# A hybrid RG-LRU / RWKV-7 layer: where the forward substitution of the second half of each pair's chunks runs

## The chip, the cores and the metric

One core of one Trainium2 chip runs the kernel. The metric is the device time of one execution in microseconds (us), a median over several runs. The engines are named as in the profile: PE is TensorE, with its weight loads as PEld; DVE is VectorE; ACT is ScalarE; POOL is GpSimd; SP is SyncE, which issues the DMAs.

## What is computed

One decoder layer over 512 tokens of width 2048. After a normalization with a conditioned shift and scale (adaLN), one projection feeds two groups of heads. The first group is a gated linear recurrence (RG-LRU). The second is RWKV-7 time mixing: 16 heads of 64 features, each with a 64 x 64 state. An output projection, a residual add, a SwiGLU sub-layer and a last normalization follow. The part that matters here is the RWKV-7 recurrence:

```python
def step(state, inp):
    r_t, d_t, k_t, v_t, kk_t, a_t = inp
    sa = jnp.einsum('bhvk,bhk->bhv', state, -kk_t)
    state = (state * d_t[:, :, None, :]
             + sa[..., None] * (kk_t * a_t)[:, :, None, :]
             + v_t[..., None] * k_t[:, :, None, :])
    y_t = jnp.einsum('bhvk,bhk->bhv', state, r_t)
    return state, y_t
```

## The kernel before

Tokens lie along the free dimension, features along the 128 partitions. Every large product is written as three matmuls on operands that were split into a high and a low part (L124, L125, L126); for that each weight tile is loaded (L115), its high part is made on ACT (L105) and its low part on DVE (L106, `wlo`). There are three buffers for the split weights.

The recurrence is computed in chunks of 64 tokens. Two heads make a pair (8 pairs); a pair has 8 chunks, built in two halves of four chunks (`rwkv_half`, hf 0 and hf 1). Within a chunk the step for `sa` is a triangular system, and `inverse` (L750) makes the inverse of I - A for the eight triangular blocks of a half (four chunks, two heads):

- L633 makes the products on PE, L635 masks them into `gb` on DVE, L637 and L639 gather the diagonal 32-blocks into `dg`, and L757 transposes these so that one 32-block lies in one partition (`at`).
- L762 to L766 are the forward substitution. Step s multiplies column s of A with row s of the inverse found so far (L764, into `pr`, shown as `rw_xp`) and adds the product to the rows below (L766, into `x`). There are 31 steps of two instructions, and each instruction takes the result of the one before it. Over the 31 steps an instruction has 31 down to 1 rows and 1 to 4 columns, 920 elements per partition in all.
- L768 and L771 transpose the result back (`xn`, `xs`). L775 copies it on POOL into the block-diagonal operand `xt` (four instructions). L783 and L793 on PE make the lower left blocks.

The chain of a pair (`rwkv_chain`, L666) then takes the eight chunks one after the other. It needs `xt` (L701) and hands the state on through DVE (L720 or L722, `rw_s`, read by PE at L696).

The order of the program is made in two stages. `weave` (L145) writes the steps of five streams (the chains, both halves, the streams' common work and the adaLN columns) into one program by a table of latencies, and fills in the large products as filler wherever no stream is due. A scheduler then puts the instructions of each engine in one list, by its own estimates, and sets the semaphores. At run time each engine goes through its list from top to bottom. POOL's list before holds memsets, the copies at L616 (`bd_a`) and those at L775.

Of the kernel before, what the change touches and what calls it, by code (L numbers as in the profile page):

```python
# [8 lines left out]
F32 = mybir.dt.float32  # L9
# [3 lines left out]
ALU = mybir.AluOpType  # L13
AX = mybir.AxisListType
PSUM = bass.MemoryType.PSUM
DRAM = bass.MemoryType.DRAM

P = 128
S = 512
# [7 lines left out]
C = 64  # L27
# [6 lines left out]
# latencies (us) that weave() goes by when it orders steps; they bear on the order only  # L34
HOP = 1.10                      # a small product, its copy out of PSUM
LM1, LM2, LM3 = 4.2, 6.8, 9.0   # the steps of rwkv_main
LH0 = 4.8                       # rwkv_half's operands
INVLAT = 30.2                   # substitution in the diagonal blocks
LSN = 1.79                      # the next state
MODLAT = (4.0, 3.8, 2.0)        # a quarter of a column of mod, by kind  # L40

# columns of the packed per-feature vectors (one column holds 128 features)
# [14 lines left out]
# columns of the constants (shapes alone)  # L57
# [29 lines left out]
class Layer:  # L87
# [24 lines left out]
    def load_split(self, src, n):  # L112
        """src: DRAM [128, n] -> (hi, lo) float32r tiles [128, n]"""
        raw = self.wp.tile([P, self.wc], F32, tag="raw", name="wraw", bufs=self.wb[0])
        self.nc.sync.dma_start(out=raw[:, :n], in_=src)  # L115
        hi = self.wp.tile([P, self.wc], F32R, tag="whi", name="whi", bufs=self.wb[1])
        lo = self.wp.tile([P, self.wc], F32R, tag="wlo", name="wlo", bufs=self.wb[1])
        with self.tc.high_priority():
            self.split_into(hi[:, :n], lo[:, :n], raw[:, :n])
        return hi, lo  # L120
# [7 lines left out]
    def gemm_steps(self, ps, src, acts):  # L128
        """ps[128, S] = W^T acts, src: DRAM [128, nk * 128], acts: list of (hi, lo); yields after each k"""
        nk = len(acts)  # L130
        kp = self.wc // P
        for k0 in range(0, nk, kp):
            kn = min(kp, nk - k0)
            hi, lo = self.load_split(src[:, k0 * P:(k0 + kn) * P], kn * P)
            for k in range(kn):
                sl = slice(k * P, (k + 1) * P)
                self.mm3(ps, (hi[:, sl], lo[:, sl]), acts[k0 + k], k0 + k == 0, k0 + k == nk - 1)
                yield
# [6 lines left out]
    def weave(self, streams, filler):  # L145
        """Traces the next step of the first stream that can run, a step of filler when none can.
        A stream yields (its last step's us on the tensor engine, the us until the next can run,
        what must hold in the trace before that); filler yields None or such a condition."""
        t = 0.0
        live = [[g, 0.0, None] for g in streams]  # L150
        fcond = None
        while live:
            for st in live:
                if st[1] <= t and (st[2] is None or st[2]()):
                    try:
                        with self.tc.issue_after(self.pe):
                            dur, lat, st[2] = next(st[0])
                        t += dur
                        st[1] = t + lat
                    except StopIteration:  # L160
                        live.remove(st)
                    break
            else:
                if filler is not None and (fcond is None or fcond()):
                    try:
                        fcond = next(filler)
                        t += 0.65
                    except StopIteration:
                        filler = None
                else:  # L170
                    t = min(st[1] for st in live if st[2] is None or st[2]())

# [1 line left out]
    def mod_pair(self, j):  # L174
        """columns j and j + 16"""
        nc = self.nc
        part = self.small.tile([P, 2], F32, tag="adapart", name="adapart", bufs=2)
        for h in range(2):
            t = self.ada.tile([P, D], F32, tag="ada", name="ada", bufs=4)
            nc.sync.dma_start(out=t, in_=self.i["w_ada"][j + 16 * h])  # L180
            nc.vector.scalar_tensor_tensor(out=t, in0=t, scalar=1.0, in1=self.cbc, op0=ALU.mult,
                                           op1=ALU.mult, accum_out=part[:, h:h + 1])
        o = _VOFF["b_ada"] + j
        nc.vector.tensor_tensor(out=self.mod[:, j:j + 17:16], in0=part, in1=self.vecs[:, o:o + 17:16],
                                op=ALU.add)

    def mod_steps(self, js, pool, tags):
        """the same for many columns, a quarter of c at a time"""
# [22 lines left out]
    def mod_scale(self, col, sc, g):  # L211
        """col = g * (1 + mod[:, sc])"""
        self.nc.vector.scalar_tensor_tensor(
            out=col, in0=self.mod[:, sc:sc + 1], scalar=1.0, in1=g, op0=ALU.add, op1=ALU.mult)

    def square(self, acc, x, k, pool):
        """acc += x * x"""
        if k == 0:
            self.nc.scalar.activation(out=acc, in_=x, func=AF.Square)
        else:  # L220
            t = pool.tile([P, S], F32, tag="ft", name="sqt", bufs=2)
            self.nc.scalar.activation(out=t, in_=x, func=AF.Square)
            self.nc.vector.tensor_tensor(out=acc, in0=acc, in1=t, op=ALU.add)

    def norm(self, acc, tag):
        """1 / rms of each token, in all partitions (PSUM), from sums of squares by partition"""
# [16 lines left out]
    def modulate(self, x, col, rstd, sh, lo=None):  # L243
        """hi, lo of x * col * rstd + sh"""
# [54 lines left out]
    def mixing(self):  # L299
# [3 lines left out]
        with ExitStack() as ctx:  # L303
            self.open_ada(ctx)
            with tc.tile_pool(name="xs", bufs=1) as xs:
# [16 lines left out]
                # seven tiles stay in PSUM, four more take turns in the last bank by quarters of K  # L322
# [43 lines left out]
    def rwkv_weave(self, kvr0, kvr1, u0):  # L366
# [16 lines left out]
        def filler():  # L383
# [15 lines left out]
            # half of the channels through the output projection  # L399
# [45 lines left out]
    def project(self, ys, half, *tags):  # L445
        """x1 += g_m * (ys through their half of w_out)"""
# [29 lines left out]
    def rwkv_setup(self, ctx):  # L476
# [4 lines left out]
        # zero at the first token of each chunk  # L481
# [3 lines left out]
        # block-diagonal operands (two heads); what lies off the blocks stays zero  # L485
# [7 lines left out]
    def lora_act(self, m, ps, pool):  # L493
        """what the second products of the low ranks take, the parts of a float32 stacked by rows:
        tanh(w) (hi, lo), a (lo, hi), all of g's first 128 rows, the other 32 (-, hi, lo, hi)"""
# [26 lines left out]
    def rwkv_main(self, pr):  # L522
        """what a pair of heads needs of all the tokens"""
# [16 lines left out]
        # decay and its running product within a chunk  # L540
# [21 lines left out]
        # kk = k * k_k over its norm per head  # L562
# [15 lines left out]
        # k' = k (1 + (a - 1) k_a), the bonus, v by tokens  # L578
# [17 lines left out]
    def rwkv_half(self, pr, hf):  # L596
        """four chunks of a pair"""
# [21 lines left out]
        # v by tokens, centred over its features  # L619
# [9 lines left out]
        # products within the chunks  # L629
# [36 lines left out]
    def rwkv_chain(self, pr):  # L666
        """a pair's state through the chunks, its output"""
# [9 lines left out]
        # through the chunks  # L677
# [49 lines left out]
        # group norm (y is centred already), bonus, gate  # L727
# [22 lines left out]
    def inverse(self, hf, dg, gb):  # L750
        """bd["xt"][hf]: the transposed inverse of I - A of each head and chunk, A^T in gb[:, :, :C]"""
# [3 lines left out]
        # diagonal 32-blocks, one to a partition (eight partitions share its columns)  # L755
# [6 lines left out]
        for s in range(31):  # L762
            n, j = 31 - s, s // 8 + 1
            tt(out=pr[:, :n, :j], in0=at[:, s + 1:, s:s + 1].to_broadcast([P, n, j]),  # L764
               in1=x[:, s:s + 1, :j].to_broadcast([P, n, j]), op=ALU.mult)
            tt(out=x[:, s + 1:, :j], in0=x[:, s + 1:, :j], in1=pr[:, :n, :j], op=ALU.add)  # L766
        xn = rw.tile([P, 32, 4], F32, tag=f"at{hf}", name="rw_xn")      # [t, j, chunk]
        nc.vector.transpose(out=xn.rearrange("p (j r) c -> p j (r c)", r=8),  # L768
                            in_=x.rearrange("p t j -> p j t"))
        xs = rw.tile([P, 4, 32], F32, tag=f"dg{hf}", name="rw_xs")      # [j, chunk, t]  # L770
# [7 lines left out]
        # lower left blocks: X21 = X22 A21 X11  # L778
# [22 lines left out]
    def lru_setup(self, ctx):  # L801
# [3 lines left out]
        # softplus(-lam) = max(-lam, 0) + 2 atanh(e / (2 + e)), e = exp(-|lam|)  # L805
# [24 lines left out]
    def lru_conv(self, j, pss=None):  # L830
        """head j: convolution"""
# [23 lines left out]
    def lru_gates(self, j):  # L855
        """gates, scan"""
# [18 lines left out]
        for m in range(2):  # L875
# [6 lines left out]
            # 1 - a^2 = tanh(-log a) (1 + a^2)  # L882
# [7 lines left out]
    def lru_gelu(self, j, pool, tags):  # L890
        """head j: its gelu branch"""
# [8 lines left out]
    def lru_out(self, j):  # L900
        """head j's product"""
# [78 lines left out]
def _tiles(w, mt=None):  # L980
    """[K, M] -> [M / 128, 128, K]: column tile m, partition p (row k * 128 + p), free (k, column)"""
# [4 lines left out]
def _pack(inp):  # L986
# [17 lines left out]
    lw = np.stack([a["lru_wa"][0], a["lru_wx"][0]], axis=1)          # [4, 2, 256, 256]  # L1004
# [41 lines left out]
```

## Time and profile before

| | us |
|---|---|
| median of three runs | 2511.34 (2509.75 to 2511.64) |
| span of the profiled execution | 2515.8 |
| PE busy in it | 2413.9 (96%) |
| DVE busy in it | 1380.4 (55%) |
| ACT busy in it | 843.7 (34%) |
| POOL busy in it | 82.0 (3%) |

The profiled execution lasted 4.5 us longer than the median of the runs. Its own time is known only as its span. The substitutions run from 224 us to 882 us of the span; what comes after about 1130 us is the SwiGLU sub-layer, in which nothing of the change lies. In rows of the timeline the columns are start, duration, engine, line, operation, output<-inputs, shape and count. In rows of groups they are count, busy time and mean duration, and behind the second bar the idle time of the engine before them.

### The profile page before, as it was taken

To read this page: it belongs to the slowest core of one execution; us is meant where nothing else is said; L and a number is where in the kernel's file an instruction comes from. 1 tells how busy PE (TensorE), PEld (TensorE's weight loads), DVE (VectorE), ACT (ScalarE), POOL (GpSimd) and SP (SyncE) were. 2 spreads that over 40 slices of the span, in tenths; PEclk is the share of its full clock that TensorE was granted. 3 is DMA by queue.
4 is the path that set the end of the run, shared out by engine and by line. 5 is a ranking of instruction groups with operands and counts; after the bars stand their busy time and mean duration, and the time that the engine had idled before them with its cause. 6 is when DMAs were issued, how large, how long until landed. Compare 5 with 4: busy or idle time off the path is not lost.

```text
span 2515.8 us, 30983 instructions
## 1 busy us (share of the span) xinstructions
PE 2413.9 (96%) x11560; PEld 1953.4 (78%) x11560; DVE 1380.4 (55%) x3111; ACT 843.7 (34%) x1340; POOL 82.0 (3%) x131
## 2 busy tenths in 40 slices
PE   5999999999999999899999999999999999999997
PEld 3677777877777886687788888888888888888885
DVE  7979898999969847854423322233322233222244
ACT  4357364455355333432222222222222222222221
POOL 0000111111101000000000000000000000000000
PEclk9999998999999999999999999999999999999998
DMA  8864444444342438366423332323333233333233
GB/s 304 308 219 130 148 128 143 131 152 144 125 135 81 143 108 283 119 195 194 160 90 95 108 100 93 101 83 98 106 98 99 89 92 105 101 93 100 85 95 112
DMA packets 138938, 333.22 MB, mean 132 GB/s; under 512 B 15458, under 2 KB 28898, under 8 KB 134690
## 3 DMA queue, kind: packets, MB, share of 16 engines
q1 hardware_dynamic: 138788, 331.25, 40.7%
q8 instruction: 90, 1.47, 0.2%
q14 instruction: 60, 0.49, 0.1%
HBM read 322.92 MB, written 7.87 MB: 131 GB/s over the span
## 4 chain that ended last, share of the span: by engine, by line
PE 72%; DVE 9%; DMA 7%; issue 1%; ACT 1%; SPq 0%; POOL 0%; DVEq 0%; ACTq 0%
PE ps_mm L124 10%; PE ps_mm L126 10%; PE ps_mm L125 10%; PE ps_gr L126 6%; PE ps_st L124 6%; PE ps_gr L124 6%; PE ps_st L126 6%; PE ps_gr L125 6%; PE ps_st L125 6%; DMA adaq<-in_w_ada 6%; DVE adaq L199 2%; DVE wlo L106 2%; DVE rw_xp L764 1%; DVE rw_x L766 1%; DMA wraw<-in_w_out 1%
## 5 line engine op out<-in xcount | busy, mean ns | idle before, releaser
L106 DVE TENSOR_TENSOR wlo<-wraw,whi 128x1024 fp32r<-128x1024 f32 (+2 forms) x552 | 496.7, 902 | 730.2 <-ACT whi L105 721.1
L105 ACT CAST whi<-wraw 128x1024 fp32r<-128x1024 f32 (+2 forms) x552 | 436.6, 792 | 1292.4 <-PE ps_mm L125 401.1
L124 PE MATMUL ps_mm<-hhi,whi 128*128 128x512 f32 x1020 | 417.1, 410 | 9.8 <-ACT hhi L251 7.2
L126 PE MATMUL ps_mm<-hhi,wlo 128*128 128x512 f32 x1020 | 407.2, 399 | 1.7 <-DVE wlo L106 1.6
L125 PE MATMUL ps_mm<-hlo,whi 128*128 128x512 f32 x1020 | 406.5, 399 | 0.8 <-DVE hlo L252 0.7
L124 PEld LDWEIGHTS ps_mm<-hhi,whi 128*128 128x128 f32 x1020 | 193.4, 190 | 53.2 <-ACT hhi L251 9.9
L125 PEld LDWEIGHTS ps_mm<-hlo,whi 128*128 128x128 f32 x1020 | 193.7, 190 | 43.4 <-DVE hlo L252 4.8
L126 PEld LDWEIGHTS ps_mm<-hhi,wlo 128*128 128x128 f32 x1020 | 193.8, 190 | 42.3 <-DVE wlo L106 3.0
L199 DVE SCALAR_TENSOR_TENSOR adaq<-adaq,cbq 128x512 f32<-128x512 f32 x256 | 173.5, 687 | 92.9 <-DMA adaq<-in_w_ada 85.1
L126 PE MATMUL ps_gr<-hhi,wlo 128*128 128x512 f32 x496 | 193.7, 390 | 3.1 <-DVE wlo L106 3.1
L126 PE MATMUL ps_st<-hhi,wlo 128*128 128x512 f32 x496 | 193.6, 390 | 2.0 <-DVE wlo L106 2.0
L124 PE MATMUL ps_st<-hhi,whi 128*128 128x512 f32 x496 | 194.0, 391 | 1.6 <-ACT hhi L251 1.6
L125 PE MATMUL ps_gr<-hlo,whi 128*128 128x512 f32 x496 | 193.5, 390 | 0.0
L125 PE MATMUL ps_st<-hlo,whi 128*128 128x512 f32 x496 | 193.5, 390 | 0.0
L124 PE MATMUL ps_gr<-hhi,whi 128*128 128x512 f32 x496 | 192.6, 391 | 0.0
L126 PEld LDWEIGHTS ps_gr<-hhi,wlo 128*128 128x128 f32 x496 | 93.4, 188 | 23.6 <-DVE wlo L106 4.1
L126 PEld LDWEIGHTS ps_st<-hhi,wlo 128*128 128x128 f32 x496 | 93.4, 188 | 21.8 <-DVE wlo L106 2.5
L124 PEld LDWEIGHTS ps_st<-hhi,whi 128*128 128x128 f32 x496 | 93.5, 188 | 21.6 <-ACT hhi L251 2.2
L125 PEld LDWEIGHTS ps_gr<-hlo,whi 128*128 128x128 f32 x496 | 93.7, 189 | 19.6
L124 PEld LDWEIGHTS ps_gr<-hhi,whi 128*128 128x128 f32 x496 | 93.7, 189 | 19.4
L125 PEld LDWEIGHTS ps_st<-hlo,whi 128*128 128x128 f32 x496 | 93.3, 188 | 19.8 <-DVE hlo L252 0.3
L766 DVE TENSOR_TENSOR rw_x<-rw_x,rw_xp 128x27 f32<-128x27 f32 (+23 forms) x496 | 94.7, 196 | 5.7
(312 smaller groups left out, 3809.6 us busy)
## 6 DMA issues: line engine op xcount, KB each, us to landing
wraw<-in_w_gu SPq DMA_DIRECT2D x176, 512.0 KB, 3.6
adaq<-in_w_ada SPq DMA_DIRECT2D x256, 256.0 KB, 3.3
wraw<-in_w_in SPq DMA_DIRECT2D x160, 256.0 KB, 3.0
ada<-in_w_ada SPq DMA_DIRECT2D x32, 1024.0 KB, 7.2
wraw<-in_w_down SPq DMA_DIRECT2D x64, 512.0 KB, 3.5
wraw<-in_w_out SPq DMA_DIRECT2D x64, 256.0 KB, 3.3
wraw<-in_w_down SPq DMA_DIRECT2D x64, 192.0 KB, 2.3
x<-in_x SPq DMA_DIRECT2D x32, 256.0 KB, 5.3
```

Source lines behind the costliest of these rows:

```text
L105: nc.scalar.copy(out=hi, in_=src)
L106: nc.vector.tensor_tensor(out=lo, in0=src, in1=hi.bitcast(F32), op=ALU.subtract)
L124: mm(ps, lhsT=w[0], rhs=x[0], start=start, stop=False)
L125: mm(ps, lhsT=w[0], rhs=x[1], start=False, stop=False)
L126: self.pe = mm(ps, lhsT=w[1], rhs=x[0], start=False, stop=stop).ins
L199: nc.vector.scalar_tensor_tensor(out=t, in0=t, scalar=1.0, in1=cb, op0=ALU.mult, op1=ALU.mult, accum_out=part[:, m, h:h + 1])
L764: tt(out=pr[:, :n, :j], in0=at[:, s + 1:, s:s + 1].to_broadcast([P, n, j]), in1=x[:, s:s + 1, :j].to_broadcast([P, n, j]), op=ALU.mult)
L766: tt(out=x[:, s + 1:, :j], in0=x[:, s + 1:, :j], in1=pr[:, :n, :j], op=ALU.add)
```

## The change

For hf 0 the 62 instructions of the substitution stay on DVE. For hf 1 they are issued on POOL. Nothing else is edited, except that comments are gone. The transposes around the substitution stay on DVE for both halves, and the latency table of `weave` is the same. From L756 on, a line of the changed kernel has a number higher by one.

```diff
         tt = nc.vector.tensor_tensor
+        gt = (nc.vector, nc.gpsimd)[hf].tensor_tensor
...
         for s in range(31):
             n, j = 31 - s, s // 8 + 1
-            tt(out=pr[:, :n, :j], in0=at[:, s + 1:, s:s + 1].to_broadcast([P, n, j]),
+            gt(out=pr[:, :n, :j], in0=at[:, s + 1:, s:s + 1].to_broadcast([P, n, j]),
                in1=x[:, s:s + 1, :j].to_broadcast([P, n, j]), op=ALU.mult)
-            tt(out=x[:, s + 1:, :j], in0=x[:, s + 1:, :j], in1=pr[:, :n, :j], op=ALU.add)
+            gt(out=x[:, s + 1:, :j], in0=x[:, s + 1:, :j], in1=pr[:, :n, :j], op=ALU.add)
```

The scheduler gives the lists another order. Three places in the last pair show it; the numbers in the names tell the buffers apart.

On DVE, the end of the last pair's second substitution before. `rw_x_8724` and `rw_xp_8726` belong to that substitution, `rw_xn_8789` is its transposed result, `wlo` rows are splits of weights:

```order
L106 TENSOR_TENSOR wlo_9061<-wraw_9058,whi_9060 128x512
L764 TENSOR_TENSOR rw_xp_8726<-rw_at_8722,rw_x_8724 128x8
L766 TENSOR_TENSOR rw_x_8724<-rw_x_8724,rw_xp_8726 128x8
L764 TENSOR_TENSOR rw_xp_8726<-rw_at_8722,rw_x_8724 128x4
L766 TENSOR_TENSOR rw_x_8724<-rw_x_8724,rw_xp_8726 128x4
L768 STREAM_TRANSPOSE rw_xn_8789<-rw_x_8724 128x128
L771 STREAM_TRANSPOSE rw_xs_8791<-rw_xn_8789 128x128
L450 SCALAR_TENSOR_TENSOR x1_8209<-ps_mm_8954,mod_90,x1_8209 128x512
L106 TENSOR_TENSOR wlo_9096<-wraw_9093,whi_9095 128x512
L720 SCALAR_TENSOR_TENSOR rw_s_9045<-ps_ch_9039,rw_pcs_7950,rw_w_9046 128x128
```

The two lines of the substitution alternate with splits and other steps down to L768. In the changed program, from the transpose that makes `rw_at_8722`, the substitution's input, to the transpose of its result:

```order
L758 STREAM_TRANSPOSE rw_at_8722<-rw_dg_8665 128x1024
L106 TENSOR_TENSOR wlo_8847<-wraw_8844,whi_8846 128x512
L740 TENSOR_TENSOR rw_t5_8683<-rw_t5_8683,rw_t4_8620 128x512
L684 TENSOR_TENSOR rw_lws_8875<-rw_w_8876,rw_lws_8875 32x128
L741 SCALAR_TENSOR_TENSOR rw_t5_8683<-rw_t5_8683,vecs_89,rw_bv_7326 128x512
L450 SCALAR_TENSOR_TENSOR x1_8206<-ps_mm_8634,mod_90,x1_8206 128x512
L106 TENSOR_TENSOR wlo_8893<-wraw_8890,whi_8892 128x512
L745 TENSOR_TENSOR rw_t5_8683<-rw_t5_8683,ps_ch_8691 128x512
L106 TENSOR_TENSOR wlo_8930<-wraw_8927,whi_8929 128x512
L450 SCALAR_TENSOR_TENSOR x1_8207<-ps_mm_8810,mod_90,x1_8207 128x512
L106 TENSOR_TENSOR wlo_8958<-wraw_8955,whi_8957 128x512
L769 STREAM_TRANSPOSE rw_xn_8789<-rw_x_8724 128x128
```

Before, 79 rows lie from L757 of this half to L768, the 62 of the substitution among them. Now it is 11 rows (L758 to L769). What stood between the substitution's rows and does not depend on it, such as the split `wlo_9061` and the state `rw_s_9045`, now stands behind L769. The first rows behind it are these:

```order
L772 STREAM_TRANSPOSE rw_xs_8791<-rw_xn_8789 128x128
L106 TENSOR_TENSOR wlo_8996<-wraw_8993,whi_8995 128x512
L722 TENSOR_SCALAR rw_s_8917<-ps_ch_8912,rw_pcs_7950 128x128
L450 SCALAR_TENSOR_TENSOR x1_8208<-ps_mm_8889,mod_90,x1_8208 128x512
L106 TENSOR_TENSOR wlo_9030<-wraw_9027,whi_9029 128x512
```

On POOL, the same half. Before, the list ends in copies:

```order
L775 TENSOR_SCALAR bd_xt0_1406<-rw_xs_7521 32x4x32 x4
L775 TENSOR_SCALAR bd_xt1_1407<-rw_xs_7709 32x4x32 x4
L616 TENSOR_SCALAR bd_a0_1394<-rw_ar_8261 64x4x64 x2
L616 TENSOR_SCALAR bd_a1_1395<-rw_ar_8593 64x4x64 x2
L775 TENSOR_SCALAR bd_xt0_1406<-rw_xs_8461 32x4x32 x4
L775 TENSOR_SCALAR bd_xt1_1407<-rw_xs_8791 32x4x32 x4
```

In the changed program the copies of hf 0 come ahead of the substitution of hf 1 here, and its own copy comes behind it:

```order
L616 TENSOR_SCALAR bd_a0_1394<-rw_ar_8261 64x4x64 x2
L616 TENSOR_SCALAR bd_a1_1395<-rw_ar_8593 64x4x64 x2
L776 TENSOR_SCALAR bd_xt0_1406<-rw_xs_8461 32x4x32 x4
L765 TENSOR_TENSOR rw_xp_8726<-rw_at_8722,rw_x_8724 128x31
L767 TENSOR_TENSOR rw_x_8724<-rw_x_8724,rw_xp_8726 128x31
L765 TENSOR_TENSOR rw_xp_8726<-rw_at_8722,rw_x_8724 128x30
```

The rest of the 62 follows in this way, each but the first waiting for the one before it, and hf 1's own copy (`bd_xt1_1407`, now L776) comes behind the last of them.

On PE, the place where the last pair's chain first reads a value that DVE makes behind its L769, `rw_s_8917`. The rows are the same in both programs:

```order
L124 MATMUL ps_mm_8889<-yhi_8194,whi_8929 128x512
L125 MATMUL ps_mm_8889<-ylo_8195,whi_8929 128x512
L126 MATMUL ps_mm_8889<-yhi_8194,wlo_8930 128x512
L694 MATMUL ps_ch_8942<-bd_v0_1402,bd_bt0_1398 128x128
L696 MATMUL ps_ch_8942<-rw_s_8917,bd_a0_1394 128x128
L124 MATMUL ps_mm_8889<-yhi_8198,whi_8929 128x512
L125 MATMUL ps_mm_8889<-ylo_8199,whi_8929 128x512
L126 MATMUL ps_mm_8889<-yhi_8198,wlo_8930 128x512
```

Before, L722 makes `rw_s_8917` 36 rows ahead of L768; in the changed program it stands three rows behind L769.

## The prediction

> **What bounds the kernel now.** I read the windows first, then the waits, then the groups of the edited lines.
>
> The windows give busy time and instructions of PE, PEld, DVE, ACT and POOL, then the granted clock. The first stretch holds the substitutions, the second is SwiGLU:
>
> ```profile
> 225.00:890.00 665.00, 636.63 (x3776) 509.55 (x3771) 582.69 (x1935) 335.52 (x656) 71.32 (x106) 0.96 0.42 131
> 1134.00:2495.00 1361.00, 1353.92 (x5967) 1118.91 (x5965) 441.96 (x525) 317.51 (x383) 0.00 (x0) 1.00 0.33 103
> ```
>
> PE works 96% of the first stretch, so time can be won there only where PE waits, and lost wherever PE is made to wait longer. DVE works 88% of it; POOL is nearly free. PE's waits in that stretch, in us, times, longest:
>
> ```profile
> PE ps_gr L783 <- DVE rw_xn L768: 18.7, 8, 3.7
> PE ps_st L568 <- ACT rw_t L566: 2.5, 2, 2.2
> ```
>
> The largest wait on DVE is the one for the substitution's result, 18.7 us. DVE's own waits there are short:
>
> ```profile
> DVE adaq L199 <- DMA adaq<-in_w_ada: 10.9, 22, 1.1
> DVE wlo L106 <- ACT whi L105: 9.8, 13, 2.1
> ```
>
> The substitution's two lines, both halves together:
>
> ```profile
> L766 DVE TENSOR_TENSOR rw_x<-rw_x,rw_xp 128x27 f32<-128x27 f32 (+23 forms) x496 | 94.7, 196 | 5.7
> L764 DVE TENSOR_TENSOR rw_xp<-rw_at,rw_x 128x27 f32<-128x27 f32 (+23 forms) x496 | 94.2, 195 | 6.0
> ```
>
> **What goes and what it can win.** Half of these instructions leave DVE: (94.7 + 94.2) / 2 = 94.5 us of its 582.7. DVE is not the bound, so of this only PE's waits for it can come back: 18.7 us, if all of them go.
>
> **What it adds: a wait inside DVE's list.** The lists in the section on the change decide this. In the last pair L769, which needs POOL's last result, is only 11 rows behind L758, which feeds POOL. In between are nine instructions of the full width of 512 and a short one. One of them in the trace:
>
> ```profile
> 883.32 0.69 DVE L106 TENSOR_TENSOR wlo<-wraw,whi 128x512 fp32r<-128x512 f32 x1
> ```
>
> Ten such rows are some 6 us of work. In the other second halves it is 12 to 27 rows, by the same durations 6 to 11 us. When DVE comes to L769 earlier than POOL is done, it stands, and with it stand the weight splits L106 and the states L720 and L722. The list fits if POOL's 62 instructions take no more than those 6 to 11 us. So the question is what they take.
>
> **POOL's price.** No two-input instruction on POOL is in this trace. The nearest rows are its copies, as groups of four and of two from start to end of a burst:
>
> ```profile
> 345.75 2.35 POOL L775 TENSOR_SCALAR bd_xt<-rw_xs 32x128 f32<-32x128 f32 x4 [10.90 <-DVE rw_xs L771]
> ...
> 821.81 1.79 POOL L616 TENSOR_SCALAR bd_a<-rw_ar 64x256 f32<-64x256 f32 x2 [13.68 <-PE ps_mm L124]
> ```
>
> 128 elements cost 2.35 / 4 = 0.588 us from start to start, 256 cost 1.79 / 2 = 0.895. That is 2.40 ns per element and 0.28 us fixed. The substitution has 920 / 31 = 29.7 elements per instruction, so 0.28 + 0.071 = 0.35 us with one input; if the second input doubles the slope, 0.42 us. I take the middle, 0.385 us: 62 x 0.385 = 24 us. The first 6 us run beside DVE's work, where POOL is slower (below); I add 1 us. So T, POOL's time for a half, is 25 us. The lower bound is DVE's own step when nothing is in between:
>
> ```profile
> 864.64 0.21 DVE L764 TENSOR_TENSOR rw_xp<-rw_at,rw_x 128x29 f32<-128x29 f32 x1
> 864.88 0.21 DVE L766 TENSOR_TENSOR rw_x<-rw_x,rw_xp 128x29 f32<-128x29 f32 x1
> ```
>
> 0.245 us from start to start, T = 15.2. The upper bound is the copy of 128 elements unscaled, 0.588 us, T = 36.4.
>
> The Trainium skill, GPSIMD Engine Reference, section Performance versus the Vector engine, speaks against the move: it states 4497 ns on GpSimd against 2293 ns on VectorE for an addition of 2048 elements, 1.96 times. By it, as an estimate, a step is 0.245 x 1.96 = 0.48 us and T = 29.8, and the sum below would come to 2650 us; the copies here put the step lower, and no run here has the instruction.
>
> **How much of T the PE hides.** PE goes on while DVE stands, until it needs something behind L769. For the last pair that is `rw_s_8917` at L696, and PE's list there is the same before and after, so the cover is read from the trace:
>
> ```profile
> 852.67 1.16 PE L633 MATMUL ps_gr<-rw_ar,bd_b 128*128 128x128 f32 x8
> ...
> 873.92 0.28 PE L696 MATMUL ps_ch<-rw_s,bd_a 128*128 128x128 f32 x1
> ```
>
> L633 ends at 853.83, L696 starts at 873.92: 20.1 us. Beside it, what DVE needs from L633 to the end of L757 in the same half:
>
> ```profile
> 857.93 2.05 DVE L757 STREAM_TRANSPOSE rw_at<-rw_dg 128x1024 f32<-128x1024 f32 x1
> ```
>
> 6.15 us, to 859.98. After POOL come two transposes of 0.40 us and the split or state that PE needs, 0.35 to 0.69 us and a row or two ahead of it: 2 us. The last pair's wait on PE is then 6.1 + 25 + 2 - 20.1 = 13 us.
>
> For the other pairs I counted the matmuls in PE's new list from L633 of the second half to the first that reads something behind its L769 (511 wide split products in all eight, at their distance in the trace, the small ones at 0.06 to 0.11 us):
>
> ```profile
> 881.24 0.39 PE L126 MATMUL ps_mm<-yhi,wlo 128*128 128x512 f32 x1
> 881.47 0.39 PE L124 MATMUL ps_mm<-yhi,whi 128*128 128x512 f32 x1
> ```
>
> At 0.23 us each the counts give 23.6, 14.8, 20.3, 16.0, 11.7, 20.5, 22.2 and 18.4 us, together 147.5. The last is 20.1 in the trace, 9% more, so I scale the sum to 161 us.
>
> The way from L633 to the end of L757 is 11.8 us in the first pair, 13.1 in the third (the longest) and 6.15 in the last; the eight add up to 70.8:
>
> ```profile
> 225.74 0.94 PE L633 MATMUL ps_gr<-rw_ar,bd_b 128*128 128x128 f32 x7
> ```
> ```profile
> 236.50 2.02 DVE L757 STREAM_TRANSPOSE rw_at<-rw_dg 128x1024 f32<-128x1024 f32 x1
> ```
> ```profile
> 414.94 0.83 PE L633 MATMUL ps_gr<-rw_ar,bd_b 128*128 128x128 f32 x6
> ```
> ```profile
> 426.80 2.06 DVE L757 STREAM_TRANSPOSE rw_at<-rw_dg 128x1024 f32<-128x1024 f32 x1
> ```
>
> In the new list there are 34 rows fewer on that way in all, nearly all substitution steps of 0.2 us, so 64 us.
>
> **The sum.** PE's new waits: 64 + 8 T + 8 x 2 - 161 = 8 T - 81, with T = 25: 119 us. Off go the 18.7 us of waits at L783, which fall inside the new ones or vanish with DVE's relief. Net 100 us. The profiled span (2515.8) is 4.5 us above the median; I add the net to the median: 2511.3 + 100 = 2611 us. With T = 15.2 the net is 22 us (2533), with T = 36.4 it is 191 (2702).
>
> What stands behind DVE has its own followers: a raw weight buffer is freed by its split, so SP's loads of `wraw` and `adaq` also pause; three split buffers are full when DVE goes on, so I count nothing for them. POOL's copies at L616 and L775 queue behind the 62 instructions. In the first two pairs hf 0's copy of `xt` is among them; PE meets it close to hf 1's place, so I count it within the same wait.
>
> **Rivals.**
>
> *POOL is quick (faster).* If an instruction takes under 100 / 8 / 62 = 0.20 us (T = 12.5), the new waits are smaller than the old. For it speaks a short row of POOL:
>
> ```profile
> L554 POOL MEMSET rw_pb<- 128x8 f32 x8 | 0.9, 113 | 0.4
> ```
>
> With the copies' gaps of (2.35 - 4 x 0.527) / 3 = 0.08 us (0.527 is their median, below) that is 0.19 us, T = 12, net -4 us: 2507 us; shorter still, the new waits vanish and the time goes to 2511.3 - 18.7 = 2493, which I take for this case. Against it: a memset reads nothing, and a copy has 0.28 us fixed. I give it 8%, 3 of them within 0.2% of no change, which is about 5 us and what a measurement of this kernel can tell.
>
> *The two engines hold each other up (slower still).* POOL's copies are not always that short. Least, median and longest of one, in ns, and a burst beside busy DVE rows:
>
> ```profile
> L775 POOL TENSOR_SCALAR bd_xt<-rw_xs x64: 517/527/1017, 275.1 to 885.0; 32x128 f32<-32x128 f32 x64
> ```
> ```profile
> 434.28 3.06 POOL L775 TENSOR_SCALAR bd_xt<-rw_xs 32x128 f32<-32x128 f32 x4 [21.09 <-DVE rw_xp L764]
> ```
> ```profile
> 434.19 0.68 DVE L199 SCALAR_TENSOR_TENSOR adaq<-adaq,cbq 128x512 f32<-128x512 f32 x1
> ...
> 434.80 0.29 DVE L766 TENSOR_TENSOR rw_x<-rw_x,rw_xp 128x29 f32<-128x29 f32 x1
> ```
>
> Four took 3.06 us instead of 2.35 there, and L766 took 0.29 instead of 0.21 us. The longest delay is 1.017 - 0.527 = 0.49 us. If every step got half of it, it would take 0.63 us, T = 39, and the time would be 2511.3 + 8 x 39 - 81 - 18.7 = 2724 us. It decides above T = 36.4. Against it: after some 6 us DVE stands and disturbs nothing. 8%.
>
> The Trainium skill, SBUF — State Buffer, section Who interferes with whom, states that a VectorE instruction with two SBUF inputs and a GpSimd one that reads SBUF block each other fully. By it, as an estimate from the rows here, the first 6 us hold 8 steps of POOL instead of 16 (half a 0.68 us instruction ahead of each), so T grows by 3 us instead of 1, to 2627 us; the burst above agrees that there is a delay.
>
> *PE has more cover than I count.* If DVE reaches L769 late anyway or PE's list runs 30% slower than its counts, the net falls below 22 us but stays positive: about 2525 us, 4%.
>
> **How the numbers follow.** The forecast, DVE standing at L769 with T between 15 and 36 us, has 80%, at 2611 us. Its bounds 2533 and 2702, rounded to 2535 and 2705, are the range; the rivals outside make the 20% left. Faster by over 0.2%: 0.05; within 0.2%: 0.03; slower: 0.80 + 0.08 + 0.04 = 0.92.
>
> **What would show it.** Right: DVE's waits have L769 waiting for POOL's L767 at the top, 8 times, 10 to 25 us each; L765 and L767 on POOL start about 0.385 us apart; PE waits for `wlo` or `rw_s` for some 119 us in all, in eight holes of 5 to 25 us. DVE's busy time in the stretch is some 95 us less. Wrong: POOL's steps under 0.2 us or over 0.6; PE's holes elsewhere, or none; a stretch from L633 to L696 in the last pair that is not longer than 20 us.

## The result and the profile after

The changed kernel takes 2621.7 us in the median against 2510.6 us for the kernel before, measured side by side: a ratio of 1.0439 (95% interval 1.0422 to 1.0455), 4.4% or some 111 us slower. A second measurement beside other runs of the kernel before gave 2621.0 against 2512.4 us, a ratio of 1.0442 (1.0420 to 1.0465), 109 us slower; the experiments below go by this pair. The forecast was 2611 us. The profile read here is that of the second measurement, with a span of 2626.1 us, because the profiled execution of the first was disturbed (3084 us, at a mean granted clock of 0.745) and is left out of the median.

The busy times of the whole execution, with their share of the span and the number of instructions:

```profile
PE 2427.3 (92%) x11560; PEld 1961.8 (75%) x11560; DVE 1329.4 (51%) x2615; ACT 841.5 (32%) x1337; POOL 233.4 (9%) x627
```

PE has the same 11560 instructions as before. Its span grew by 110.3 us (from 2515.8) and its busy time by 13.4 (from 2413.9). So PE stood for 96.9 us more, and it took 13.4 us more for the same work.

The windows of the changed kernel, one over the substitutions and one in SwiGLU (columns as in the prediction):

```profile
225.00:1000.00 775.00, 647.99 (x3782) 519.45 (x3782) 530.79 (x1443) 334.88 (x654) 222.99 (x602) 0.91 0.36 112
1250.00:2610.00 1360.00, 1353.45 (x5967) 1118.50 (x5965) 442.13 (x525) 318.92 (x385) 0.00 (x0) 1.00 0.32 102
```

The stretch with the substitutions carries nearly all of the loss: PE is busy 84% of it, at a granted clock of 0.91 (the share of its full speed that PE was granted). In SwiGLU nothing moved: the same 5967 matmuls, 1353.5 us against 1353.9.

DVE's waits in the stretch, in us, times, longest:

```profile
DVE rw_xn L769 <- POOL rw_x L767: 118.6, 8, 16.3
DVE adaq L199 <- DMA adaq<-in_w_ada: 28.5, 34, 2.5
DVE wlo L106 <- ACT whi L105: 18.5, 19, 2.9
```

The first row did not exist before: DVE stands once in each pair at the transpose that needs POOL's last result. PE's waits in the same stretch:

```profile
PE ps_ch L696 <- DVE rw_s L720: 51.4, 7, 14.9
PE ps_gr L784 <- DVE rw_xn L769: 22.4, 4, 18.0
PE ps_st L568 <- ACT rw_t L566: 17.7, 2, 15.2
PE ps_ch L696 <- DVE rw_s L722: 10.8, 1, 10.8
PE ps_mm L126 <- DVE wlo L106: 10.6, 2, 10.0
```

PE has eight holes of 8 to 18 us, one in each pair, about 100 us together. In four it lacks a state from L720, in the last one a state from L722, in one the transpose itself, in one a split, and in one (873 to 889 us) a result of ACT. The timeline shows that this one too leads to DVE:

```profile
881.01 0.40 DVE L772 STREAM_TRANSPOSE rw_xs<-rw_xn 128x128 f32<-128x128 f32 x1
...
884.95 1.22 DVE L551 TENSOR_TENSOR_SCAN rw_t<-keep,rw_t 128x512 f32<-128x512 bf16 x1
...
886.21 0.63 ACT L555 ACTIVATE rw_pb<-rw_t 128x512 f32<-128x512 f32 x1 [16.34 <-DVE rw_t L551]
```

L551 stands in DVE's list behind L769, and ACT, which had stood for 16.3 us for L551, comes to L566, for which PE waits, only after that.

The last pair from the products to the state, the place at which the prediction read its cover:

```profile
952.77 1.16 PE L633 MATMUL ps_gr<-rw_ar,bd_b 128*128 128x128 f32 x8
...
958.04 2.06 DVE L758 STREAM_TRANSPOSE rw_at<-rw_dg 128x1024 f32<-128x1024 f32 x1
960.25 0.55 POOL L765 TENSOR_TENSOR rw_xp<-rw_at,rw_x 128x31 f32<-128x31 f32 x1 [3.91 <-DVE rw_at L758]
...
983.01 0.20 POOL L767 TENSOR_TENSOR rw_x<-rw_x,rw_xp 128x4 f32<-128x4 f32 x1
983.25 0.40 DVE L769 STREAM_TRANSPOSE rw_xn<-rw_x 128x128 f32<-128x128 f32 x1 [14.07 <-POOL rw_x L767]
...
984.58 0.34 DVE L722 TENSOR_SCALAR rw_s<-ps_ch,rw_pcs 128x128 f32<-128x128 f32 x1
984.98 0.80 PE L696 MATMUL ps_ch<-rw_s,bd_a 128*128 128x128 f32 x2 [10.79 <-DVE rw_s L722]
```

From the end of L633 (953.93) to L696 it was 20.1 us before; now it is 31.05: 6.2 us to the end of L758 (960.10), 23.1 for POOL, 1.8 for the transposes, a split and the state. PE's cover is used up 10.8 us before the end.

### The profile page after: what moved, and what is told of

Same layout as the page of the kernel before. It is cut to its first block, busy times and chain, and to the rows that moved or that the text cites. A ratio compares the mean times of both kernels' runs of the same rounds, so it can differ in the third digit from the quotient of the medians.

```text
span 3081.9 us, 31023 instructions
## 1 busy us (share of the span) xinstructions
PE 2956.9 (96%) x11560; PEld 2100.3 (68%) x11560; DVE 1334.2 (43%) x2615; ACT 847.6 (28%) x1337; POOL 231.4 (8%) x627
## 4 chain that ended last, share of the span: by engine, by line
PE 84%; POOL 5%; DVE 3%; issue 2%; DMA 1%; ACT 0%; SPq 0%; DVEq 0%; POOLq 0%; ACTq 0%
PE ps_mm L126 12%; PE ps_mm L124 12%; PE ps_mm L125 12%; PE ps_st L125 7%; PE ps_gr L124 7%; PE ps_st L124 7%; PE ps_gr L126 7%; PE ps_gr L125 7%; PE ps_st L126 7%; POOL rw_x L767 3%; POOL rw_xp L765 2%; PE ps_gr L633 1%; PE ps_gr L643 1%; PE ps_ch L696 1%; PE ps_ch L701 1%
## 5 line engine op out<-in xcount | busy, mean ns | idle before, releaser
L124 PE MATMUL ps_mm<-hhi,whi 128*128 128x512 f32 x1020 | 483.8, 476 | 6.5 <-ACT hhi L251 5.2
L126 PE MATMUL ps_mm<-hhi,wlo 128*128 128x512 f32 x1020 | 476.0, 467 | 8.1 <-DVE wlo L106 8.1
L125 PE MATMUL ps_mm<-hlo,whi 128*128 128x512 f32 x1020 | 470.8, 462 | 0.0
L124 PEld LDWEIGHTS ps_mm<-hhi,whi 128*128 128x128 f32 x1020 | 209.5, 206 | 86.7 <-ACT hhi L251 6.9
L125 PE MATMUL ps_st<-hlo,whi 128*128 128x512 f32 x496 | 229.2, 462 | 0.0
L124 PE MATMUL ps_gr<-hhi,whi 128*128 128x512 f32 x496 | 227.7, 462 | 0.0
L124 PE MATMUL ps_st<-hhi,whi 128*128 128x512 f32 x496 | 225.1, 454 | 1.6 <-ACT hhi L251 1.6
L125 PE MATMUL ps_gr<-hlo,whi 128*128 128x512 f32 x496 | 225.8, 455 | 0.0
L126 PE MATMUL ps_st<-hhi,wlo 128*128 128x512 f32 x496 | 225.7, 455 | 0.0
L126 PE MATMUL ps_gr<-hhi,wlo 128*128 128x512 f32 x496 | 224.4, 452 | 0.0
L199 DVE SCALAR_TENSOR_TENSOR adaq<-adaq,cbq 128x512 f32<-128x512 f32 x256 | 173.1, 691 | 73.1 <-DMA adaq<-in_w_ada 66.5
L124 PEld LDWEIGHTS ps_st<-hhi,whi 128*128 128x128 f32 x496 | 100.5, 203 | 44.6 <-ACT hhi L251 2.2
L124 PEld LDWEIGHTS ps_gr<-hhi,whi 128*128 128x128 f32 x496 | 97.3, 196 | 42.0
L124 PE MATMUL ps_gr<-shi,whi 128*128 128x512 f32 x242 | 110.7, 457 | 0.0
```

The lines of the kernel that those rows point to most:

```text
L124: mm(ps, lhsT=w[0], rhs=x[0], start=start, stop=False)
L125: mm(ps, lhsT=w[0], rhs=x[1], start=False, stop=False)
L126: self.pe = mm(ps, lhsT=w[1], rhs=x[0], start=False, stop=stop).ins
```

## The experiments

Two theories are told apart. The list: POOL's 62 instructions in themselves do little harm; the loss is the wait for their result in DVE's fixed list, behind which splits and states stand. Collision: POOL and DVE slow each other down when they work at the same time. A third, the late inverse, comes in further down: PE lacks POOL's result itself, wherever the wait for it stands. All times are medians over three rounds or more, beside runs of the kernel before on the same chip (its medians were 2512.4, 2511.7 and 2512.7 us in the three groups of runs).

### The same kernel again

No edit.

> The changed kernel once more, for a profile at the full clock. By every theory 2620 to 2625 us. The theory of the list (VectorE stands at the transpose L769 until GpSimd is done, and the splits and states behind it starve TensorE) expects: VectorE's wait of L769 for L767 at the top of its waits, 8 times, some 100 us in all; GpSimd's steps about 0.385 us apart on the mean, T about 24 us; holes on TensorE of 5 to 20 us in every pair, about 100 us more waiting than before. The theory of collision (the two engines hold each other up at SBUF, whoever waits) expects VectorE's own instructions longer in total by tens of us instead.

2621.0 us, as expected; its profile is the one above, with DVE's wait for L767 at the top, as the theory of the list had it.

### What the relief of DVE is worth alone

The second halves keep one of the 31 steps, on DVE. This leaves 30 of their 31 steps out of the output.

```diff
-        gt = (nc.vector, nc.gpsimd)[hf].tensor_tensor
+        gt = nc.vector.tensor_tensor
...
-        for s in range(31):
+        for s in range(1 if hf else 31):
```

> The second halves keep one of their 31 steps, on VectorE; 30 steps are left out, and nothing runs on GpSimd instead. What the relief of VectorE alone can give. The theory of the list expects 2488 to 2505 us: at most the 18.7 us that TensorE waits at L783 come back. A rival by which VectorE's load bounds the stage expects about 2511 - 90 = 2420 us. The difference between this run and the one without a wait is the price of collision: by the theory of the list under 15 us, by the theory of collision over 60 us.

2503.5 us, a ratio of 0.9964 (0.9950 to 0.9978). Its largest wait of PE in the stretch:

```profile
PE ps_gr L784 <- DVE rw_xn L769: 7.4, 5, 2.3
```

With the second halves' substitution all but gone, 9 us are to be had. A placement on another engine at best comes near that. The rival by which DVE's load bounds the stage, with 2420 us, fell.

### Half of POOL's steps

Every second step of the second halves is left out, so the output lacks them; the other steps run on POOL.

```diff
-        for s in range(31):
+        for s in range(0, 31, 1 + hf):
```

> The changed kernel with every second step of the second halves left out: 32 instructions on GpSimd instead of 62, VectorE's transposes still wait for them. T falls from 24 to about 12.5 us. The theory of the list expects the sum 8 T - 81 - 18.7 to give 2511 us by its straight line; pairs whose cover is longer than their wait can't win more than their wait, so 2510 to 2530 us. The theory of collision expects half of the loss, about 2565 us.

2561.1 us, 1.0195 (1.0175 to 1.0215). This lies near what collision expected and far above what the theory of the list did. Its wait of DVE:

```profile
DVE rw_xn L769 <- POOL rw_x L767: 63.2, 8, 8.7
```

POOL's T was 12.5 us in the mean of the eight halves. DVE stood for 63.2 / 8 = 7.9 of these, so it had only 4.6 us of work in between. The order shows why: the transpose stands closer behind L758 in this program. Up to it lie 7 or 8 rows that are no steps of a substitution, where it was 10 to 14; the scheduler has probably reckoned with the shorter substitution. The straight line through T had kept the list fixed; it moves with T. So this run does not tell the theories apart, and the expectation of the list failed for its own reason.

### Nothing waits for POOL's result

The second halves' substitution is left out of the output here and in the next two kernels: all 62 instructions run on POOL, but they read the masked products, and the transposes take a constant.

```diff
-            gt(out=pr[:, :n, :j], in0=at[:, s + 1:, s:s + 1].to_broadcast([P, n, j]),
+            gt(out=pr[:, :n, :j], in0=src(s).to_broadcast([P, n, j]),
...
-                            in_=x.rearrange("p t j -> p j t"))
+                            in_=(self.con("xinit").rearrange("p (t j) -> p t j", j=4) if hf else x)
+                            .rearrange("p t j -> p j t"))
```

> GpSimd runs the 62 instructions of every second half as in the changed kernel, of the same shapes, but on a stand-in (the mask product gb), and VectorE's transposes read a constant, so nothing waits for GpSimd's result; the substitution of the second halves is thereby left out of the output. GpSimd starts some 6 us earlier in a half. The theory of the list expects the loss to vanish: 2490 to 2520 us, since the relief of VectorE stays and only the collision is left to pay. The theory of collision expects 2560 us or more, since the same 496 instructions still run beside VectorE's, now even beside a VectorE that never stands.

2615.8 us, 1.0418 (1.0402 to 1.0433): hardly less than the changed kernel. DVE's longest wait says that the edit had missed its aim:

```profile
DVE rw_x L761 <- POOL rw_x L776: 109.4, 7, 17.5
```

L761 fills the buffer `x` for the second half of the next pair. It must wait until POOL is done with the buffer, and the scheduler had put it early in DVE's list. The wait of 118.6 us at L769 had become one of 109.4 at L761, and the time stayed. This was not meant. That DVE stands as long at another instruction and the time hardly changes fits the theory of the list; collision, with its 2560 us or more, is not refuted by this run.

In the next kernel POOL fills its own buffer, and substitutes after the copies of `xt`:

```diff
-        nc.vector.tensor_copy(out=x.rearrange("p t j -> p (t j)"), in_=self.con("xinit"))
+        (nc.vector, nc.gpsimd)[hf].tensor_copy(out=x.rearrange("p t j -> p (t j)"), in_=self.con("xinit"))
...
+        if hf:
+            substitute()
         yield 0, INVLAT, None
```

> All 62 instructions of POOL for each second half run, with the same shapes, but nothing that PE or DVE needs soon depends on them: POOL reads the masked products, also fills its own buffer and substitutes only after the copies of xt, and the transposes take a constant in place of its result. The second halves' substitution is thereby left out of the output. No instruction of DVE's list waits for the substitution for more than an instant. The theory of the list: 2490 to 2520 us, about the time of the kernel whose second halves kept one step on DVE (2503.5), although POOL works as long as in the changed kernel. Collision: 2560 us or more, DVE's wide rows longer than 0.69 us by a tenth or more, and POOL's T far above 24 us.

2539.8 us, 1.0113 (1.0091 to 1.0135): most of the loss is gone, but 28 us are left, more than the list expected and less than collision did. The first row of PE's waits names the larger part of them:

```profile
PE ps_ch L701 <- POOL bd_xt L790: 17.9, 2, 15.4
```

This is a queue on POOL itself. The copies of `xt` for the first half stood behind the 62 instructions of the second half. The last kernel of this line moves them to DVE:

```diff
-            nc.gpsimd.tensor_scalar(out=xt[rows, :, rows], in0=xs[rows], scalar1=1.0,
+            (nc.vector, nc.gpsimd)[hf].tensor_scalar(out=xt[rows, :, rows], in0=xs[rows], scalar1=1.0,
```

> The kernel in which nothing waits for POOL's substitution (2539.8 us), with one more edit: the four copies of xt of the first half run on DVE, so that nothing that PE needs soon stands behind the 62 instructions in POOL's list. As there, the second halves' substitution is left out of the output. Queue theory (the 28 us that were left over the kernel before came from copies of the first half behind POOL's substitution: PE waited 17.9 us at L701 for them): the two waits at L701 go, 2512 to 2524 us. Collision theory (POOL slows DVE down as both read and write): the loss stays, 2535 us or more.

2518.7 us, 1.0026 (1.0016 to 1.0037), as expected if the rest came from the copies. POOL works more than in the changed kernel, and the time is 6 us above the kernel before. Its windows and its groups on POOL:

```profile
225.00:1000.00 775.00, 732.33 (x4238) 585.14 (x4235) 596.61 (x1581) 366.53 (x716) 246.86 (x577) 0.96 0.44 137
```

```profile
L777 POOL TENSOR_TENSOR rw_x<-rw_x,rw_xp 128x24 f32<-128x24 f32 (+23 forms) x248 | 97.0, 391 | 19.5
L775 POOL TENSOR_TENSOR rw_xp<-rw_gb,rw_x 128x24 f32<-128x24 f32 (+23 forms) x248 | 95.0, 383 | 130.8 <-DVE rw_at L758 96.7 <-DVE rw_xp L775 9.1 <-DVE rw_x L777 6.2
```

PE is busy 732 us of the stretch, against 648 in the changed kernel. The collision is in the groups: with DVE at work beside it all the time, an instruction of POOL takes 0.39 us, in the changed kernel 0.31 and 0.30. DVE's own wide rows notice little, here a split of 512 columns between 225 and 960 us:

```profile
L106 DVE TENSOR_TENSOR wlo<-wraw,whi 128x512 fp32r<-128x512 f32 x161 | 111.7, 694 | 57.4 <-ACT whi L105 52.4 <-PE ps_ch L709 2.0 <-PE ps_mm L126 0.9
```

It takes 694 ns in the mean, and 686 in the kernel before; the 60 of these splits that start while POOL substitutes take 705. From the first to the last of POOL's 62 instructions it is 31.6 us (mean of the eight), in the changed kernel 23.5. Of these 8 us more, 2.9 are the half's four copies of `xt` (L790), which stand between the steps here, and 5.2 are slower steps. But nobody waits for that here. Of the 2621.0 - 2512.4 = 109 us of the changed kernel, 6 remain; measured from the kernel without the second halves' work (2503.5), POOL's work beside DVE costs 15.

So collision is not the bulk of the loss. But this kernel takes away every use of POOL's result, and not only the place in DVE's list at which it is awaited. What that place alone is worth has to be seen with the result in use.

### The result is needed, but the transposes stand further down

The changed kernel, with the transposes traced 30 or 36 us later and placed behind the split that was traced last. POOL's 62 instructions and their use are all there. The last line of the edit takes the added delay out of the time that `weave` reckons with behind the transposes.

```diff
-        nc.vector.tensor_tensor(out=lo, in0=src, in1=hi.bitcast(F32), op=ALU.subtract)
+        self.dve = nc.vector.tensor_tensor(out=lo, in0=src, in1=hi.bitcast(F32), op=ALU.subtract).ins
...
+        yield 0, 30.0 if hf else 0, None
+        with self.tc.issue_after(self.dve) if hf else ExitStack():
...
-        yield 0, INVLAT, None
+        yield 0, 4.2 if hf else INVLAT, None
```

> The changed kernel, with the two transposes behind the second half's substitution traced 30 us later, so that in DVE's list 30 to 46 rows lie between L758 and the transpose that needs POOL (16 in two pairs) in place of 11 to 13. POOL's 62 instructions are all there. The theory of the list (the loss is DVE standing at that transpose): DVE's wait for POOL falls from 118.6 us to under 40, PE's busy time returns to about 2414 us, and the time is 2500 to 2535 us, most of the loss gone. Collision (POOL and DVE slow each other down): now POOL runs beside working DVE rows for its whole length, T goes well above 24 us, DVE's own rows lengthen, and the time is 2580 us or more. Late inverse (PE needs the second half's inverse itself, wherever the transposes stand): PE waits at L784 and L701 in place of L696, and the time stays near 2600 us.

2569.0 us, 1.0219 (1.0198 to 1.0241).

> The same with 36 us: 41 to 51 rows lie between in six pairs, 33 and 15 in the last two. The theory of the list: the wait of DVE for POOL is nearly gone in the first six pairs, 2495 to 2520 us; the relief of DVE alone was worth 9 us, so nothing under 2490. Late inverse: the chain gets its operand 36 us after the substitution began, PE waits at L784 or L701, and the time is higher than with 30 us. Collision: 2580 us or more, as with 30 us.

2557.9 us, 1.0179 (1.0161 to 1.0198). DVE's wait for POOL's substitution in this kernel:

```profile
DVE rw_xn L771 <- POOL rw_x L767: 7.9, 5, 2.2
```

The wait has gone from 118.6 to 7.9 us, and with it 62 of the 109 us (with 30 us: 6.2 us of wait, 51 us won). PE's busy time is 2413.0 us again, as in the kernel before, so what is left is waiting. No expected time was met. Those of the list were too good: they counted no other place at which POOL could hold something up. Collision expected 2580 us or more, and the late inverse a time near 2600 us that rises with the delay; it fell. PE's longest waits with 36 us are three:

```profile
PE ps_ch L701 <- POOL bd_xt L778: 15.4, 2, 13.0
PE ps_mm L124 <- ACT yhi L105: 11.9, 3, 10.0
PE ps_ch L694 <- DVE rw_t L737: 10.3, 1, 10.3
```

The first is the queue on POOL again. The longest of the second lies at 966 to 977 us, behind the last pair: ACT's cast there waits 9.1 us for the load of `y`, which the last pair's chain has just written, and PE has nothing else to do. The third is a queue on POOL too, of another kind. L737 stands in DVE's list behind L890, a step of the RG-LRU. L890 waits for a memset of one column on POOL (L888), and the memset stands amid the 62 instructions:

```profile
563.77 0.10 POOL L888 MEMSET lru_ulo<- 128x1 f32 x1
563.90 0.69 DVE L890 TENSOR_TENSOR lru_g<-lru_g,lru_ulo 128x512 f32<-128x512 f32 x1 [8.47 <-POOL lru_ulo L888]
...
566.39 0.72 DVE L737 SCALAR_TENSOR_TENSOR rw_t<-ps_ch,eps,rw_t 128x512 f32<-128x512 f32 x1
```

So of the 33 us in the longest three waits, 23 come from other work in POOL's list. The rest of the 46 us was not taken apart. POOL's T is 29.5 us here; what that longer T costs, no run shows.

Two more kernels add cures to the one with 30 us: first the first half's copies of `xt` on DVE, then in addition the last pair's second half on DVE as before.

> The changed kernel with the transposes 30 us later (2569.0 us) and the four copies of xt of the first half on DVE. Queue theory: PE's wait of 10 us at L701 in the second pair goes, and 15 to 25 us of the loss with it: 2540 to 2555 us; what is left is the last pair, whose chain ends later, and second halves whose inverse comes late. Collision: no change, 2565 us or more.

2556.3 us, 1.0167 (1.0141 to 1.0193), 13 us less than without the copies on DVE. That is just above the upper end of what the queue theory had (2555); the wait at L701 for the copies is gone from PE's waits.

```diff
+        self.n1 = getattr(self, "n1", 0) + hf
+        pool = bool(hf and self.n1 < 8)
+        gt = (nc.vector, nc.gpsimd)[pool].tensor_tensor
```

> The same, with the last pair's second half substituted on DVE as in the kernel before. If the rest of the loss lies in the last pair's late end (PE waited 8.6 us at L124 there and worked at half clock after it), the time falls by a further 10 to 15 us, to 2525 to 2545 us; if it is spread over the pairs, by less than 5. Below 2505 us it would beat the kernel before; the relief of DVE alone gave 2503.5.

2545.2 us, 1.0131 (1.0114 to 1.0148), a further 11 us, as expected if the last pair's late end costs that. What is left, 33 us over the kernel before, is spread over PE's waits, none longer than 6 us:

```profile
PE ps_gr L788 <- DVE rw_xn L773: 12.5, 5, 3.1
PE ps_ch L696 <- DVE rw_s L720: 11.3, 7, 5.8
PE ps_mm L124 <- DVE mix_r L472: 7.3, 2, 4.8
```

This rest was not taken apart further.

### Both halves on POOL

The kernel with 30 us, with `gt = nc.gpsimd.tensor_tensor` and the late transposes for both halves.

> Both halves' substitutions on POOL, with the transposes 30 us later for both. DVE is relieved of all 992 instructions; POOL has 16 times some 24 us = 380 us of work in the 660 us of the stretch. The theory of the list: DVE's wait stays small if the rows between (13 to 48) cover T, and the time lies between 2490 and 2560 us; where POOL has both halves queued one behind the other, T as DVE sees it doubles, and the wait returns there. Collision: over 2600 us.

2572.7 us, 1.0247 (1.0223 to 1.0270), above the upper end of what the theory of the list expected (2560) and below collision's 2600. DVE waited 37.4 us for POOL's substitutions, and PE's longest waits lay elsewhere: 13.9 us at L655, 10.0 at L124, 9.2 at L732. The first leads back to POOL, by the same memset as above:

```profile
DVE lru_g L890 <- POOL lru_ulo L888: 39.6, 6, 13.1
```
```profile
245.25 0.10 POOL L888 MEMSET lru_ulo<- 128x1 f32 x1
...
245.38 0.69 DVE L890 TENSOR_TENSOR lru_g<-lru_g,lru_ulo 128x512 f32<-128x512 f32 x1 [13.13 <-POOL lru_ulo L888]
...
246.74 0.63 ACT L887 ACTIVATE lru_ulo<-lru_ulo 128x512 f32<-128x512 f32 x1 [14.26 <-DVE lru_ulo L886]
247.39 0.58 ACT L657 COPY rw_bn<-ps_st 128x512 f32<-128x512 f32 x1
...
248.03 1.11 PE L655 MATMUL ps_st<-cons,bd_k 128*128 128x128 f32 x4 [13.92 <-ACT rw_bn L657]
```

The memset takes 0.10 us, but it stands in POOL's list behind a substitution, and DVE, ACT and PE stand in turn. DVE's waits for it in the stretch were 3.4 us in the kernel before and are 39.6 us here. The other two of PE's waits were not followed. None of the kernels that keep the whole computation beats the kernel before.

## Why the prediction was right

**The mechanism.** DVE stands at L769 eight times, 118.6 us in all, and PE runs dry behind it, as forecast. The free kernel with the copies moved shows that POOL's work in itself is not the loss: it stays, everything that waits for it goes, and 102 of the 109 us go too. The kernel with the transposes 36 us later shows the wait in DVE's list itself: POOL's result stays in use, DVE's wait for it falls to 7.9 us, and 62 of the 109 us go. The other 46 us of that kernel are explained in part: 23 us by other work in POOL's list. The rival of a quick POOL fell, as T is nowhere near 12.5 us, and so did that of more cover, as the net loss is far from 22 us.

**POOL's price.** Forecast: 0.385 us from start to start, T = 25. The groups of the changed kernel, busy time and mean:

```profile
L767 POOL TENSOR_TENSOR rw_x<-rw_x,rw_xp 128x24 f32<-128x24 f32 (+23 forms) x248 | 76.6, 309 | 19.4
L765 POOL TENSOR_TENSOR rw_xp<-rw_at,rw_x 128x24 f32<-128x24 f32 (+23 forms) x248 | 73.5, 296 | 72.1 <-DVE rw_at L758 38.9 <-DVE rw_xp L765 8.2 <-DVE rw_x L767 6.2
```

From start to start it is 0.37 to 0.41 us in the mean of a half, 0.33 in the median, and T from the end of L758 is 22.8 to 25.5 us, 23.7 in the mean. So T was met, but not by the right parts. The undisturbed step of 0.333 us lies below even the 0.35 that the copies gave for one input; the middle of 0.385 was 16% too high, which is 3 us of T. The first steps, next paragraph, made up for 2 of them. The Trainium skill, GPSIMD Engine Reference, section Performance versus the Vector engine, would have given 29.8, as an estimate: its ratio of 1.96 is measured at 2048 elements, and here, at 30, POOL's median step is 0.333 / 0.245 = 1.36 times DVE's.

**The collision at the start.** I had added 1 us for the first 6 us beside DVE's work. At the median step of 0.333 the 62 would take 20.6 us; T is 23.7, so it is 3 us. The first twelve steps take 0.46 to 0.76 us each in the mean of a half, the last thirty 0.32. That is what the rule of the Trainium skill, SBUF — State Buffer, section Who interferes with whom, gave as an estimate. The delay is uneven here, though: POOL's steps grow from 0.32 to 0.46 us and more, while the 16 splits of 512 columns that start beside them take 713 ns in the mean, the others 689. As a rival, with half of the longest delay on every step, it fell: DVE stands and leaves POOL alone.

**The cover and the sum.** The terms as they came, for the eight pairs together: from L633 to the end of L758 66.7 us (forecast 64), POOL's T 189.4 (200), from POOL's end to what PE needs 24 (16), PE's cover 180 (161). The cover is what the eight ways from L633's end to the end of the hole, 280 us in all, leave beside the 100 us of holes, so the sum of these terms closes by itself; the forecast had 119. For the last pair, whose cover was read from the trace, the forecast was 13 and it came to 11; the covers counted in matmuls were too short by a tenth.

**What goes.** Of the 18.7 us of waits at L783 before, I let all fall; the row at L784 above still has 22.4 - 18.0 = 4.4 us beside its hole. So the sum gives 100 - 14.3 = 86 us; PE stood for 96.9 more. The other 11 us are smaller waits that I did not itemise.

**What was missing.** The forecast held PE's work itself constant. It grew by 13.4 us, as shown at the start. With 96.9 it makes the 110.3 us of the span. So 2611 against 2622 is in part luck, as errors cancelled: the sum had 19 us too much in the new waits, and it lacked 4.4 us of old waits that stay, 11 us of smaller ones and 13.4 us of slower matmuls.

**DVE's busy time.** Forecast: 95 us less. The two lines did lose 94.7 + 94.2 - 50.0 - 49.6 = 89 us of durations, but DVE's busy time fell by only 1380.4 - 1329.4 = 51. An instruction of DVE can start before the one ahead of it has ended: in the rows of the prediction L766 starts at 434.80, while L199 runs until 434.87. The 992 rows of the two lines before last 194 us in all, but without them DVE's busy time would have been only 108 us shorter; half of that is 54. The forecast did not rest on it.

**The followers on POOL.** I counted nothing for the copies behind the 62 instructions, as PE would meet them in the same hole. In the changed kernel that holds: PE's wait at L701 for `bd_xt` is 1.2 us. Where the holes are gone it does not: moving those copies to DVE won 21 us in the free kernel and 13 in the one with later transposes.

## What to carry to other kernels

Before a dependent chain goes to an idle engine, count the rows between the instruction that feeds it and the first that needs it, on every engine that works through a list: what lies between must be longer than the chain on the new engine, and if it is not, all that is queued behind stands. Look also at what stands in the idle engine's own list behind the chain, however short it is, and at buffers that are handed on only when it is done. And ask first what the relief can bring: here it was 9 us, because the relieved engine was not the bound.

## What the runs showed of the hardware

PE's clock is lower right after a hole, so a wait costs more than its length. Behind the last pair's hole of 10.8 us in the changed kernel the wide matmuls start 0.43 us apart, and 4.9 us later 0.23 us:

```profile
984.98 0.80 PE L696 MATMUL ps_ch<-rw_s,bd_a 128*128 128x128 f32 x2 [10.79 <-DVE rw_s L722]
...
986.00 0.63 PE L125 MATMUL ps_mm<-ylo,whi 128*128 128x512 f32 x1
986.43 0.63 PE L126 MATMUL ps_mm<-yhi,wlo 128*128 128x512 f32 x1
...
989.84 0.39 PE L124 MATMUL ps_mm<-yhi,whi 128*128 128x512 f32 x1
990.07 0.39 PE L125 MATMUL ps_mm<-ylo,whi 128*128 128x512 f32 x1
```

The windows give the granted clock (third number from the end) behind the second pair's hole and behind the last pair's, and in the 10 us after that:

```profile
385.70:395.89 10.19, 9.68 (x53) 6.74 (x54) 4.44 (x12) 5.00 (x11) 5.83 (x8) 0.50 0.32 104
984.98:989.84 4.86, 4.86 (x14) 3.99 (x14) 1.35 (x2) 1.55 (x4) 1.63 (x4) 0.50 0.22 77
989.84:1000.00 10.16, 10.16 (x59) 8.83 (x58) 2.75 (x5) 2.34 (x6) 0.00 (x0) 1.00 0.22 68
```

Behind each of the eight holes PE works at half its clock: for 2.8 to 5.2 us behind six of them, for 10.2 and 12.5 us behind two. Over the stretch PE was busy at half clock for 71.5 us, and for 46.0 in the kernel before; the 25.5 us more account for 12.8 of the 13.4 us by which its busy time grew. That the granted clock of the stretch fell as far as from 0.97 to 0.91 is half due to the holes themselves: 73 of the 147 us at half clock lie in them.

The Trainium skill, TensorE: Matmul & The Clock Gate, section Part 1: The HAM clock gate, states that after an idle window of about 3.4 us PE runs at half rate until it has been busy for about as long. The half rate agrees, and so, roughly, does its length behind six holes; behind the other two it lasted three times as long, with PE busy 94% of the time or more. By it, as an estimate, eight holes cost 8 x 3.4 / 2 = 13.6 us. That this comes so near 13.4 is luck: the half clock lasted 46 us behind the holes, which cost some 22 us, and elsewhere there was less of it than in the kernel before. The prediction had the eight holes and did not ask what follows them. That the holes cause the slower clock was not tried by itself, and the kernel before has 48 us of half clock in its stretch although no hole of PE there lasts 4 us.
